# Sliding attention by query blocks of all eight heads, with the values as stationary operand

## The chip, the cores and the metric

The kernel runs on one core of one Trainium2 chip. The metric is the device time of one launch in microseconds. Three runs of the kernel before gave 2348.06 us in the median (2347.34 to 2348.9). A core has TensorE (PE: matmuls and transposes), VectorE (DVE), ScalarE (ACT), GpSimd (POOL) and the DMA queue of SyncE (SP); they work side by side and wait for one another through semaphores. Matmuls read SBUF and write PSUM, of which the kernel uses 8 banks of 128 partitions x 512 fp32.

## The reference

512 tokens of width 1024 go through one block of a first kind and two layers of a second kind. The first block, cut to what the change touches:

```python
qa, ka, va, qb, kb, vb, ga, gb = jnp.split(rmsnorm(x, g) @ w_in, offsets, axis=-1)
oa = dilated_attention(qa, ka, va)              # 12 heads of 64, three dilations
qb = apply_partial_rope(rmsnorm(qb), cos, sin)  # 8 query heads of 64
kb = apply_partial_rope(rmsnorm(kb), cos, sin)  # 2 key heads: four query heads share one
# query block i of 128 sees key blocks i-1 and i, window 128, and a sink logit per head
m = jnp.maximum(jnp.max(s, axis=-1, keepdims=True), sk)
p = jnp.exp(s - m)
denom = jnp.sum(p, axis=-1, keepdims=True) + jnp.exp(sk - m)
o = jnp.einsum('bnjhgqk,bnjkhd->bnjqhgd', p / denom, vb)
mix = sigmoid(ga) * (oa @ w_branch_a) + sigmoid(gb) * (ob @ w_branch_b)
x = x + mix @ w_out                             # then an MLP of width 4096
```

A layer of the second kind is an FFN, a mixer of three branches (stick-breaking attention "sb", a causal softmax attention "mla", a gated linear recurrence "ml") and a second FFN.

## The kernel before

All weight products run with weights and activations split in a high and a low part (three matmuls each, in the format fp32r); attention products and transposes run in fp32. load_w brings weights by SP's DMA (wraw), ScalarE rounds them (whi), VectorE subtracts (wlo).

The order of TensorE is written out by a planner, the class Loom. It carries a model time, now, to which each matmul and transpose adds a fixed price:

```python
self.loom.now += n * 4.17e-4 if rhs.dtype == F32R else 2 * max(0.107, n * 8.34e-4)
```

Attention work is written as jobs that yield either a delay in this model time (T_EXP between scores and transposes, T_PT 1.9 between transposes and value product, T_HEADS 10 and 16 between a projection and the transposes of its heads) or a condition. Between two matmuls of the streamed weight products the planner steps every job that is due. Many conditions ask for room in the slot store H: ND = 18 slots "D" of 4352 bytes a partition, and NB = 5 slots "B" of 2048 bytes, which hold transposed weights (pT in block 1, mpT of mla in block 2) and other small tiles. The order on ScalarE, VectorE, GpSimd and SP is set by the tile scheduler.

Sliding attention is the job swa(tb, kvh): eight units of one query block tb (128 queries) and one key head kvh with its four query heads; the generator attend does most of it. Scores s go to PSUM, VectorE adds the mask and takes the maximum (p), ScalarE forms the exponentials and their sums (den). PE transposes p in pieces of 128x128 (pT), ScalarE and VectorE copy them, and the value product swo has the transposed weights as stationary operand and the values, 64 columns, moving: eight matmuls for two key blocks, four for the first query block. VectorE multiplies the 128x256 result by 1/den, and a second job (o_job) transposes it back (oT), whence ScalarE copies it to ob. Four units wait for kb and qb0, four for kb and qb1. After them come the dilated units (dil_unit), which need the transposed heads q0T and k0T (tile hT) of the projections that run meanwhile.

In block 2 the names are: sbs, the scores of sb; sbl, its triangular sums, with a carry by VectorE between them; sbo, its value product; mls, mlT, mlo: scores, transposes and value product of mla; pf and pt: streamed projections.

Of the kernel before, what the change touches and what calls it, by code (L numbers as in the profile page):

```python
# [9 lines left out]
F32 = mybir.dt.float32  # L10
# [8 lines left out]
D = 1024  # L19
KB = 8  # L20
TB = 4
# [7 lines left out]
def dram(t, off, ap):  # L29
    return bass.AP(tensor=t.tensor, offset=t.offset + off, ap=ap)  # L30
# [96 lines left out]
class Net:  # L127
    def __init__(self, ctx, tc, a):
        self.tc, self.nc, self.a = tc, tc.nc, a
        P = lambda name, bufs, **k: ctx.enter_context(tc.tile_pool(name=name, bufs=bufs, **k))  # L130
        self.const = P("const", 1)
        self.wp = P("wp", 2)
        self.act = P("act", 1)
        self.sc = P("sc", 2)
        self.tiny = P("tiny", 2)
        self.ps = P("ps", 8, space=PSUM)
        ctx.enter_context(tc.manual_schedule(engines={mybir.EngineType.PE}))
        self.loom = Loom()
        self.H = Slots(self.act, [("B", 2048, NB), ("D", 4352, ND)], self.loom.wait)
        self.dr = P("dr", 1, space=bass.MemoryType.DRAM)  # L140
        self.x = self.act.tile([128, KB, S], F32, name="x")
        self.xh = self.act.tile([128, KB, S], F32R, name="xh")
        self.xl = self.act.tile([128, KB, S], F32R, name="xl")
        self.xs = [(self.xh[:, k], self.xl[:, k]) for k in range(KB)]
        self.held = []
        self.normed = False
        self.make_consts()


# [178 lines left out]
            self.hg[n] = t  # L328


    def load_w(self, w, ncol, r0, kb, c0, nc_, c1=None):


        nc = self.nc
        halves = [c0] if c1 is None else [c0, c1]
        w_ = nc_ * len(halves)
        step = max(1, 1024 // w_)
        out = []
        for k0 in range(0, kb, step):
            kn = min(step, kb - k0)  # L340
            raw = self.wp.tile([128, kn * w_], F32, name="wraw", tag="wraw", bufs=WB[0])
            hi = self.wp.tile([128, kn * w_], F32R, name="whi", tag="whi", bufs=WB[1])
            lo = self.wp.tile([128, kn * w_], F32R, name="wlo", tag="wlo", bufs=WB[1])
            rv = raw.rearrange("p (k c) -> p k c", c=w_)
            for i, c in enumerate(halves):
                nc.sync.dma_start(rv[:, :, i * nc_:(i + 1) * nc_],
                                  dram(w, (r0 + k0 * 128) * ncol + c, [[ncol, 128], [128 * ncol, kn], [1, nc_]]))
            nc.scalar.copy(hi, raw)  # L348
            nc.vector.tensor_sub(lo, raw, hi.bitcast(F32))  # L349
            out += [(hi[:, k * w_:(k + 1) * w_], lo[:, k * w_:(k + 1) * w_]) for k in range(kn)]  # L350
        return out
# [279 lines left out]
            nc.scalar.activation(o, ps, AF.Copy, scale=gain)  # L631


    def attend(self, q, k, heads, qs, ks, nb, mask, mcol, dcol, v, ops, sink=None):


        nc = self.nc
        n = nb * 128
        yield lambda: self.H.room(4096)
        p = self.tok("p4")  # L640
        for g in range(2):
            ps = self.bank("s").rearrange("p (h n) -> p h n", n=256)
            for i in range(2):
                h, kv = heads[2 * i + g]
                hs = slice(g * 64, g * 64 + 64)
                self.mm(ps[:, i, 0:n], q[h // 2][hs, qs], k[kv][hs, ks], True, True)
            for i in range(2):
                j = 2 * i + g
                nc.vector.tensor_tensor_reduce(p[:, j, 0:n], ps[:, i, 0:n], mask, scale=0.125, scalar=-3e38,
                                               op0=ALU.add, op1=ALU.max, accum_out=mcol[:, j:j + 1])  # L650
        if sink is not None:
            nc.vector.tensor_max(mcol, mcol, sink)
        nm = self.tiny.tile([128, 4], F32, name="nm", tag="nm", bufs=4)
        nc.vector.tensor_scalar(nm, mcol, -1.0, None, op0=ALU.mult)
        for j in range(4):
            nc.scalar.activation(p[:, j, 0:n], p[:, j, 0:n], AF.Exp, bias=nm[:, j:j + 1], accum_out=dcol[:, j:j + 1])
        if sink is not None:
            e = self.tiny.tile([128, 4], F32, name="es", tag="es", bufs=4)
            nc.vector.tensor_add(e, nm, sink)
            nc.scalar.activation(e, e, AF.Exp)  # L660
            nc.vector.tensor_add(dcol, dcol, e)
        yield T_EXP[nb]
        per = 4 // nb
        yield lambda: self.H.room(2048, 2048)
        pts = []
        for g in range(nb):
            tp = self.bank("pT").rearrange("p (n c) -> p n c", c=128)
            for i in range(4):
                j, b = g * per + i // nb, i % nb
                self.tr(tp[:, i], p[:, j, b * 128:(b + 1) * 128], self.ident)  # L670
            pt = self.blk("pT")
            pts.append(pt)
            if g % 2:
                nc.vector.tensor_copy(pt, tp.rearrange("p n c -> p (n c)"))
            else:
                nc.scalar.copy(pt, tp.rearrange("p n c -> p (n c)"))
        self.H.put(p)
        yield T_PT
        o = ops()
        for g in range(nb):  # L680
            for i in range(4):
                j, b = g * per + i // nb, i % nb
                self.mm(o[:, j], pts[g][:, i * 128:(i + 1) * 128], v(j, b), b == 0, b == nb - 1)
        self.H.put(*pts)

    def o_out(self, o, tb, ys, n):

# [33 lines left out]
    def block1(self):  # L721
        nc, a, T, H, loom = self.nc, self.a, self.tiny, self.H, self.loom
        w = a["w_in"][0]
# [9 lines left out]
        kv = self.tok("kvb")  # L733
# [6 lines left out]
        with self.tc.manual_schedule(engines={mybir.EngineType.DVE, mybir.EngineType.Activation}):  # L740
# [10 lines left out]
            for b in range(TB):  # L751
                ps = self.bank("pt")[:, 0:256]
# [16 lines left out]
        sinks = self.bcast_row(a["sinks"][0], 8, "sinks")  # L769
# [15 lines left out]
        ready = set()  # L785
# [32 lines left out]
        kbT = [kbt[:, 0], kbt[:, 1]]  # L818
        out = {}
# [15 lines left out]
        loom.add(rows_job())  # L835
        two(2304, 2560, 0, ("qb", "qb"), ("qb0", "qb1"))
        ob = [self.duo("ob") for _ in range(2)]
        left = {"swa": 8, "obT": 8, 0: 4, 1: 4, 2: 4}
        units = []

        def swa(tb, kvh):
            nb = 1 if tb == 0 else 2
            ks = slice((tb + 1 - nb) * 128, (tb + 1) * 128)
            m = T.tile([128, 4], F32, name="swm", tag="swm", bufs=4)
            den = T.tile([128, 4], F32, name="swd", tag="swd", bufs=4)
            box = []

            def ops():
                box.append(self.bank("swo").rearrange("p (h d) -> p h d", d=64)[:, 0:4])
                return box[0]  # L850
            qbT = [out[f"qb{i // 2}"][:, i % 2] if i // 2 == kvh else None for i in range(4)]
            yield from self.attend(qbT, kbT, [(h, kvh) for h in range(kvh * 4, kvh * 4 + 4)],
                                   slice(tb * 128, (tb + 1) * 128), ks, nb, self.band[1][:, 256 - nb * 128:256], m, den,
                                   lambda j, b: kv[:, tb + 1 - nb + b, 128 + kvh * 64:192 + kvh * 64], ops,
                                   sinks[:, kvh * 4:kvh * 4 + 4])
            nc.vector.reciprocal(den, den)
            yield lambda: H.room(1024)
            o = H.get("swo", [128, 256])
            nc.vector.tensor_mul(o.rearrange("p (h d) -> p h d", d=64), box[0], den.unsqueeze(2).to_broadcast([128, 4, 64]))

            def done():
                left["obT"] -= 1
            loom.add(self.o_job(o, tb, [ob[kvh]], 2, 2.0, done))
            left["swa"] -= 1
            if left["swa"] == 0:
                H.put(kv, kbt, out.pop("qb0"), out.pop("qb1"))
        for kvh in range(2):
            for tb in range(TB):
                units.append((lambda kvh=kvh: {"kb", f"qb{kvh}"} <= ready, lambda tb=tb, kvh=kvh: swa(tb, kvh)))


        va, og = [], {}
# [99 lines left out]
        wb = a["w_branch_b"][0]  # L972
        for m in range(KB):
            if m % 4 == 0:
                bp = self.load_w(wb, D, 0, 4, m * 128, 512)
            self.after(nc.scalar.activation(mix[m], mix[m], AF.Sigmoid), last)
            pb = self.bank("pbr")
            self.fm(bp, obs, m % 4, pb)
            nc.vector.tensor_mul(mix[m], mix[m], pb)
# [3 lines left out]
        wb = a["w_branch_a"][0]  # L983
        mp = []
        for m in range(KB):
# [3 lines left out]
            if m % 4 == 0:  # L989
                bp = self.load_w(wb, D, 0, 2, m * 128, 512)  # L990
# [618 lines left out]
T_KD, T_HEADS, T_EXP, T_PT = 22.0, (10.0, 16.0), {1: 4.5, 2: 6.5}, 1.9  # L1609
# [30 lines left out]


ND, NB, SCR = 18, 5, 6
WB = (2, 4)
```

## Time and profile before

| | |
|---|---|
| median of three runs | 2348.06 us |
| profiled execution | 2348.01 us |
| its span | 2346.3 us |
| TensorE busy | 2331.9 us, 99% |
| VectorE, ScalarE, GpSimd busy | 1275.5, 905.1, 381.3 us |

The span runs from the first to the last instruction of the profiled execution. Block 1's attention lies in the first 300 us; the mixers of the two layers of block 2 have their attention at about 1000 to 1110 and 1800 to 1910 us. A row of the timeline gives start, duration, engine, line, operation, tile written and tiles read, shapes and the number of merged records. An fp32 matmul or transpose leaves one record or two, by its kind; the x numbers count records.

### The profile page before, as it was taken

To read this page: it belongs to the slowest core of one execution; us is meant where nothing else is said; L and a number is where in the kernel's file an instruction comes from. 1 tells how busy PE (TensorE), PEld (TensorE's weight loads), DVE (VectorE), ACT (ScalarE), POOL (GpSimd) and SP (SyncE) were. 2 spreads that over 40 slices of the span, in tenths; PEclk is the share of its full clock that TensorE was granted. 3 is DMA by queue.
4 is the path that set the end of the run, shared out by engine and by line. 5 is a ranking of instruction groups with operands and counts; after the bars stand their busy time and mean duration, and the time that the engine had idled before them with its cause. 6 is when DMAs were issued, how large, how long until landed. Compare 5 with 4: busy or idle time off the path is not lost.

```text
span 2346.3 us, 28790 instructions
## 1 busy us (share of the span) xinstructions
PE 2331.9 (99%) x11064; PEld 1946.7 (83%) x11064; DVE 1275.5 (54%) x2214; ACT 905.1 (39%) x1510; POOL 381.3 (16%) x385
## 2 busy tenths in 40 slices
PE   8999999999999999999999999999999999999999
PEld 7899888888888888877888888888888778888887
DVE  7744556435355545785554554455458755446552
ACT  6645433222223223676333333223236572333321
POOL 2000014101022112211111321211211110113110
PEclk9999999999999999999999999999999999999999
DMA  4212432333323323322233333333232232323332
GB/s 137 64 55 73 121 96 90 101 97 95 103 86 100 101 92 98 87 65 85 72 90 99 99 95 94 94 95 99 90 101 82 72 86 58 105 81 108 91 102 87
DMA packets 250462, 213.71 MB, mean 91 GB/s; under 512 B 14166, under 2 KB 234068, under 8 KB 250324
## 3 DMA queue, kind: packets, MB, share of 16 engines
q1 hardware_dynamic: 250324, 211.87, 30.4%
q8 instruction: 87, 1.43, 0.2%
q14 instruction: 51, 0.42, 0.1%
HBM read 208.64 MB, written 3.19 MB: 90 GB/s over the span
## 4 chain that ended last, share of the span: by engine, by line
PE 98%; DMA 1%; ACT 0%; DVE 0%; SPq 0%; issue 0%; ACTq 0%
PE pd L175 15%; PE pgate L175 15%; PE pt L175 15%; PE pg L175 10%; PE pa L175 10%; PE pu L175 7%; PE pf L175 6%; PE po L175 5%; PE pbr L175 5%; PE mls L175 1%; PE sbs L175 1%; PE mnum L175 1%; PE sbl L175 1%; PE mss L175 1%; PE mlo L175 1%; PE s L175 1%
## 5 line engine op out<-in xcount | busy, mean ns | idle before, releaser
L349 DVE TENSOR_TENSOR wlo<-wraw,whi 128x1024 fp32r<-128x1024 f32 (+3 forms) x394 | 546.5, 1387 | 415.3 <-ACT whi L348 411.3
L348 ACT CAST whi<-wraw 128x1024 fp32r<-128x1024 f32 (+3 forms) x394 | 404.6, 1028 | 666.7 <-PE pg L175 141.9
L175 PE MATMUL pd<-hidh,whi 128*128 128x512 f32 x520 | 202.3, 389 | 0.0
L175 PE MATMUL pd<-hidl,whi 128*128 128x512 f32 x520 | 202.3, 389 | 0.0
L175 PE MATMUL pd<-hidh,wlo 128*128 128x512 f32 x520 | 202.3, 389 | 0.0
L175 PE MATMUL pgate<-xh,whi 128*128 128x512 f32 x512 | 201.2, 393 | 0.0
L175 PE MATMUL pgate<-xh,wlo 128*128 128x512 f32 x512 | 199.4, 390 | 0.0
L175 PE MATMUL pgate<-xl,whi 128*128 128x512 f32 x512 | 199.3, 389 | 0.0
L175 PE MATMUL pt<-whi,xh 128*128 128x512 f32 (+2 forms) x480 | 182.0, 379 | 0.0
L175 PE MATMUL pt<-whi,xl 128*128 128x512 f32 (+2 forms) x480 | 172.8, 360 | 0.0
L175 PE MATMUL pt<-wlo,xh 128*128 128x512 f32 (+2 forms) x480 | 172.5, 359 | 0.0
L175 PE MATMUL pa<-xl,whi 128*128 128x512 f32 x352 | 137.2, 390 | 0.7 <-DVE xl L438 0.7
L175 PE MATMUL pa<-xh,whi 128*128 128x512 f32 x352 | 137.6, 391 | 0.0
L175 PE MATMUL pg<-xh,whi 128*128 128x512 f32 x352 | 137.4, 390 | 0.0
L175 PE MATMUL pa<-xh,wlo 128*128 128x512 f32 x352 | 137.1, 389 | 0.0
L175 PE MATMUL pg<-xh,wlo 128*128 128x512 f32 x352 | 137.0, 389 | 0.0
L175 PE MATMUL pg<-xl,whi 128*128 128x512 f32 x352 | 137.0, 389 | 0.0
L549 POOL TENSOR_TENSOR t<-t,t 128x512 f32<-128x512 f32 x44 | 56.7, 1290 | 426.5 <-ACT whi L348 303.8
L175 PEld LDWEIGHTS pd<-hidh,wlo 128*128 128x128 f32 x520 | 97.6, 188 | 20.4
L175 PEld LDWEIGHTS pd<-hidl,whi 128*128 128x128 f32 x520 | 97.6, 188 | 20.3
L175 PEld LDWEIGHTS pd<-hidh,whi 128*128 128x128 f32 x520 | 97.6, 188 | 20.1
L175 PEld LDWEIGHTS pgate<-xh,wlo 128*128 128x128 f32 x512 | 96.1, 188 | 20.3
(488 smaller groups left out, 4671.2 us busy)
## 6 DMA issues: line engine op xcount, KB each, us to landing
wraw<-in_w_in_dram SPq DMA_DIRECT2D x116, 512.0 KB, 3.6
wraw<-in_ffn_wi_dram SPq DMA_DIRECT2D x176, 256.0 KB, 3.0
wraw<-in_ffn_wo_dram SPq DMA_DIRECT2D x34, 512.0 KB, 3.5
wraw<-in_w_up_dram SPq DMA_DIRECT2D x32, 512.0 KB, 3.8
wraw<-in_w_out_dram SPq DMA_DIRECT2D x24, 512.0 KB, 3.4
wraw<-in_w_down_dram SPq DMA_DIRECT2D x24, 512.0 KB, 3.9
wraw<-in_w_in_dram SPq DMA_DIRECT2D x32, 256.0 KB, 2.9
wraw<-in_ffn_wo_dram SPq DMA_DIRECT2D x12, 384.0 KB, 3.1
```

The lines of the kernel that those rows point to most:

```text
L175: self.nc.tensor.matmul(out, lhsT, rhs, start=start, stop=stop)
L348: nc.scalar.copy(hi, raw)
L349: nc.vector.tensor_sub(lo, raw, hi.bitcast(F32))
L549: nc.gpsimd.tensor_mul(t2, t2, t1)
```

## The change

Sliding attention becomes four units, one for each query block, with all eight heads (the new method weigh does scores and exponentials, turned the transposes and their copy, which goes to ScalarE and VectorE in turn). VectorE multiplies the weights p by 1/den before they are transposed. The value product takes the values (128x64) as stationary operand and the transposed weights, 512 columns of four heads, as the moving one; key head 0 writes partitions 0 to 63 and key head 1 partitions 64 to 127 of one bank, in turn. The result stands transposed, so the transposes oT and their job are gone and ScalarE copies it to ob. Since ob now has its rows in another order, load_w brings the rows of w_branch_b in two halves of 64 partitions (eight DMAs of half the size for four). A unit waits for kb, qb0 and qb1. NB goes from 5 to 9, for the whole program.

```diff
+            if part:
+                for i in range(2):
+                    nc.sync.dma_start(rv[i * 64:i * 64 + 64],
+                                      dram(w, (r0 + i * part + k0 * 64) * ncol + c0, [[ncol, 64], [64 * ncol, kn], [1, nc_]]))
+                halves = []
...
+    def turned(self, p, jb):
+
+        nc = self.nc
+        tp = self.bank("pT").rearrange("p (n c) -> p n c", c=128)
+        for i, (j, b) in enumerate(jb):
+            self.tr(tp[:, i], p[:, j, b * 128:(b + 1) * 128], self.ident)
+        pt = self.blk("pT")
+        self.odd = not self.odd
+        (nc.scalar.copy if self.odd else nc.vector.tensor_copy)(pt, tp.rearrange("p n c -> p (n c)"))
+        return pt
...
-        def swa(tb, kvh):
+        def swa(tb):
...
-            nc.vector.reciprocal(den, den)
-            yield lambda: H.room(1024)
-            o = H.get("swo", [128, 256])
-            nc.vector.tensor_mul(o.rearrange("p (h d) -> p h d", d=64), box[0], den.unsqueeze(2).to_broadcast([128, 4, 64]))
-
-            def done():
-                left["obT"] -= 1
-            loom.add(self.o_job(o, tb, [ob[kvh]], 2, 2.0, done))
+            for kvh in range(2):
+                yield lambda: H.room(4096)
+                m = T.tile([128, 4], F32, name="swm", tag="swm", bufs=4)
+                den = T.tile([128, 4], F32, name="swd", tag="swd", bufs=4)
+                q = [out[f"qb{kvh}"][:, i % 2] for i in range(4)]
+                p = self.weigh(q, kbT, [(h, kvh) for h in range(kvh * 4, kvh * 4 + 4)], ts, ks, nb,
+                               self.band[1][:, 256 - nb * 128:256], m, den, sinks[:, kvh * 4:kvh * 4 + 4])
+                nc.vector.reciprocal(den, den)
+                pv = p[:, :, 0:nb * 128]
+                nc.vector.tensor_mul(pv, pv, den.unsqueeze(2).to_broadcast([128, 4, nb * 128]))
+                ps.append(p)
+                yield 1.0
+            yield T_EXP[nb] + 1.0
+            yield lambda: H.room(*[2048] * (2 * nb))
+            pts = [[self.turned(p, [(j, b) for j in range(4)]) for b in range(nb)] for p in ps]
+            H.put(*ps)
+            yield T_PT
+            o = self.bank("swo")
+            for b in range(nb):
+                for kvh in range(2):
+                    c = 128 + kvh * 64
+                    self.mm(o[kvh * 64:kvh * 64 + 64], kv[:, tb + 1 - nb + b, c:c + 64], pts[kvh][b], b == 0, b == nb - 1)
+            H.put(*sum(pts, []))
+            for i in range(2):
+                nc.scalar.copy(ob[i][:, :, ts], o[:, i * 256:i * 256 + 256].rearrange("p (n c) -> p n c", c=128))
...
-            units.append((lambda kvh=kvh: {"kb", f"qb{kvh}"} <= ready, lambda tb=tb, kvh=kvh: swa(tb, kvh)))
+            units.append((lambda: {"kb", "qb0", "qb1"} <= ready, lambda tb=tb: swa(tb)))
...
-                bp = self.load_w(wb, D, 0, 4, m * 128, 512)
+                bp = self.load_w(wb, D, 0, 4, m * 128, 512, part=256)
...
-ND, NB, SCR = 18, 5, 6
+ND, NB, SCR = 18, 9, 6
```

The order on TensorE moves at two kinds of places. The first is in block 1, where the heads of the first dilation, q0 and k0 (tile qk), are transposed into hT. Before, at the end of the sliding units of the second key head:

```order
L175 MATMUL pt<-whi,xl 128x256
L182 MATMUL pT<-ident,p_1166 128x128 x4
L175 MATMUL swo<-kvb,pT 128x64 x8
L175 MATMUL s<-kbT,qb1T 128x256 x4
L175 MATMUL swo<-kvb,pT 128x64 x4
L175 MATMUL s<-kbT,qb1T 128x256 x4
L182 MATMUL hT<-ident,qk 128x128 x16
```

Five of the eight units' value products have been done by then. Now, with only the first of four units done (swo x2 is its value product, the x4 that of the second):

```order
L176 MATMUL swo<-pT,kvb 64x512 x2
L176 MATMUL s<-kbT,qb0T 128x256 x4
L183 MATMUL pT<-ident,p_918 128x128 x8
L183 MATMUL pT<-ident,p_978 128x128 x8
L176 MATMUL s<-kbT,qb1T 128x256 x4
L183 MATMUL hT<-ident,qk 128x128 x8
L176 MATMUL swo<-pT,kvb 64x512 x4
L176 MATMUL s<-kbT,qb0T 128x256 x4
L183 MATMUL hT<-ident,qk 128x128 x8
```

The transposes of q0 moved ahead of the second unit's value product, and no streamed matmul stands among these rows.

The second place is in the mixers of block 2, the same in both layers: the last query block of mla (its scores mls, transposes mlT, value products mlo) beside the second head pair of sb. Before, on TensorE:

```order
L175 MATMUL mlo<-mv,mpT 128x64 x4
L175 MATMUL mls<-mhT 128x512
L175 MATMUL mlo<-mv,mpT 128x64 x3
L175 MATMUL pt<-whi,xh 128x512
L175 MATMUL pt<-wlo,xh 128x512
L175 MATMUL pt<-whi,xl 128x512
...
L182 MATMUL mlT<-ident,mp 128x128 x4
```

Behind the dots three more streamed matmuls stand, and from there on the transposes, value products and sums come singly, each with six or more streamed matmuls (pt) between. Now, from the last scores of sb's second head pair to the last value product of mla:

```order
L176 MATMUL sbs<-sbq,sbk 128x512
L183 MATMUL mlT<-ident,mp 128x128 x12
L176 MATMUL pf<-xh,whi 128x512
...
L176 MATMUL mlo<-mv,mpT 128x64 x4
L176 MATMUL mls<-mhT 128x512
L176 MATMUL mlo<-mv,mpT 128x64 x8
L183 MATMUL oT<-ident,mo 128x128 x2
L183 MATMUL mlT<-ident,mp 128x128 x4
L176 MATMUL sbl<-sbp,trigt 128x128
L176 MATMUL sbl<-sbp_8593,trigt 128x256
L176 MATMUL mlo<-mv,mpT 128x64 x4
```

Behind the dots stand eleven more matmuls of pf; three heads are transposed at once, and the value products, scores and sums behind pf follow one another with no streamed matmul between.

## Rows read from the trace of the kernel before

**Rows 1.** The page: the span, busy time by engine, the chain's shares by engine.
```profile
span 2346.3 us, 28790 instructions
...
PE 2331.9 (99%) x11064; PEld 1946.7 (83%) x11064; DVE 1275.5 (54%) x2214; ACT 905.1 (39%) x1510; POOL 381.3 (16%) x385
...
PE 98%; DMA 1%; ACT 0%; DVE 0%; SPq 0%; issue 0%; ACTq 0%
```

**Rows 2.** All that TensorE waited for: total us, times, longest us.
```profile
PE colT L182 <- DMA rows<-in_ln_g_dram: 4.7, 1, 4.7
PE xtp L182 <- DMA xin<-in_x_dram: 4.0, 1, 4.0
PE pa L175 <- DVE xl L438: 0.7, 1, 0.7
PE po L175 <- DVE mxl L527: 0.6, 1, 0.6
PE pT L182 <- ACT q0T L631: 0.2, 1, 0.2
```

**Rows 3.** Timeline of TensorE (start us, duration us), block 1's sliding attention.
```profile
80.58 1.89 PE L175 MATMUL swo<-kvb,pT 128*128 128x64 f32 x16
82.40 1.14 PE L175 MATMUL s<-kbT,qb0T 64*128 64x256 f32 x8
...
101.09 1.97 PE L182 MATMUL hT<-ident,qk 128*128 128x128 f32 x16
```

**Rows 4.** Timeline of TensorE, the stick-breaking value product of layer 1.
```profile
1033.48 0.39 PE L175 MATMUL pf<-xh,wlo 128*128 128x512 f32 x1
1033.80 2.37 PE L175 MATMUL sbo<-sbz,sbv 128*64 128x512 f32 x16
1036.10 2.42 PE L175 MATMUL sbs<-sbq,sbk 64*128 64x384 f32 x8
```

**Rows 5.** Timeline of TensorE, one fp32 score matmul of 512 columns (mls).
```profile
1058.29 1.08 PE L175 MATMUL mls<-mhT 96*128 96x512 f32 x2
1059.21 0.78 PE L175 MATMUL mlo<-mv,mpT 128*128 128x64 f32 x6
```

**Rows 6.** Timeline of TensorE, a pair of transposes back among streamed matmuls.
```profile
92.57 0.38 PE L182 MATMUL oT<-ident,swo 128*128 128x128 f32 x2
92.70 0.36 PE L175 MATMUL pt<-whi,xh 128*128 128x256 f32 x1
92.91 0.28 PE L175 MATMUL pt<-wlo,xh 128*128 128x256 f32 x1
```

**Rows 7.** Timeline of VectorE, q0's normalising product and its last rotary step.
```profile
91.95 1.22 DVE L791 TENSOR_TENSOR qk<-qk,rh16y 128x1024 f32<-128x1024 f32 x1
...
94.14 0.42 DVE L622 TENSOR_TENSOR qk<-ru,rv 128x256 f32<-128x256 f32 x1
```

**Rows 8.** Timeline of ScalarE, layer 1: an sb exponential; the score copies' start; mla's exponential.
```profile
1031.87 1.05 ACT L1411 ACTIVATE sbz<-sbz 128x1024 f32<-128x1024 f32 x1
...
1037.33 0.60 ACT L1380 ACTIVATE sbz<-sbs 128x512 f32<-128x512 f32 x1 [0.50 <-PE sbs L175]
...
1042.29 0.54 ACT L1319 ACTIVATE mp<-mp,mnm 128x256 f32<-128x256 f32 x1
```

**Rows 9.** Timelines of TensorE and VectorE: a triangular sum and its carry.
```profile
1026.13 0.81 PE L175 MATMUL sbl<-sbp,trigt 128*128 128x384 f32 x2
...
1027.24 0.54 DVE L1405 TENSOR_TENSOR sbp<-sbl,sbt 1x384 f32<-1x384 f32 x1
```

**Rows 10.** Timeline of TensorE after the wait that ends at 10.88 us.
```profile
14.35 0.41 PE L175 MATMUL pt<-whi,xl 128*128 128x256 f32 x1
14.56 0.41 PE L175 MATMUL pt<-whi,xh 128*128 128x256 f32 x1
...
15.15 0.28 PE L175 MATMUL pt<-whi,xh 128*128 128x256 f32 x1
15.26 0.28 PE L175 MATMUL pt<-wlo,xh 128*128 128x256 f32 x1
```

More of the change, by code (lines that the diff above doesn't have):

```diff
@@ L146, in __init__ @@
         self.normed = False
+        self.odd = False
         self.make_consts()
@@ L328, in rope2, with load_w @@
             self.hg[n] = t
-    def load_w(self, w, ncol, r0, kb, c0, nc_, c1=None):
+    def load_w(self, w, ncol, r0, kb, c0, nc_, c1=None, part=None):
         nc = self.nc
@@ L631, in heads_T, with weigh @@
             nc.scalar.activation(o, ps, AF.Copy, scale=gain)
-    def attend(self, q, k, heads, qs, ks, nb, mask, mcol, dcol, v, ops, sink=None):
+    def weigh(self, q, k, heads, qs, ks, nb, mask, mcol, dcol, sink=None):
         nc = self.nc
         n = nb * 128
-        yield lambda: self.H.room(4096)
         p = self.tok("p4")
@@ L661, in attend @@
             nc.vector.tensor_add(dcol, dcol, e)
+        return p
+    def turned(self, p, jb):
[7 more added lines that the diff above has]
+        return pt
+    def attend(self, q, k, heads, qs, ks, nb, mask, mcol, dcol, v, ops):
+        H = self.H
+        yield lambda: H.room(4096)
+        p = self.weigh(q, k, heads, qs, ks, nb, mask, mcol, dcol)
         yield T_EXP[nb]
         per = 4 // nb
[L664 to L677, printed above, removed]
+        yield lambda: H.room(2048, 2048)
+        self.odd = False
+        pts = [self.turned(p, [(g * per + i // nb, i % nb) for i in range(4)]) for g in range(nb)]
+        H.put(p)
         yield T_PT
@@ L683, in attend @@
                 self.mm(o[:, j], pts[g][:, i * 128:(i + 1) * 128], v(j, b), b == 0, b == nb - 1)
-        self.H.put(*pts)
+        H.put(*pts)
     def o_out(self, o, tb, ys, n):
@@ L837, in block1 @@
         ob = [self.duo("ob") for _ in range(2)]
-        left = {"swa": 8, "obT": 8, 0: 4, 1: 4, 2: 4}
+        left = {"swa": 4, 0: 4, 1: 4, 2: 4}
         units = []
-        def swa(tb, kvh):
+        def swa(tb):
             nb = 1 if tb == 0 else 2
             ks = slice((tb + 1 - nb) * 128, (tb + 1) * 128)
[L844 to L855, printed above, removed]
-            nc.vector.reciprocal(den, den)
-            yield lambda: H.room(1024)
-            o = H.get("swo", [128, 256])
-            nc.vector.tensor_mul(o.rearrange("p (h d) -> p h d", d=64), box[0], den.unsqueeze(2).to_broadcast([128, 4, 64]))
-            def done():
-                left["obT"] -= 1
-            loom.add(self.o_job(o, tb, [ob[kvh]], 2, 2.0, done))
@@ new lines, in swa @@
+            ts = slice(tb * 128, (tb + 1) * 128)
+            ps = []
+            for kvh in range(2):
+                yield lambda: H.room(4096)
+                m = T.tile([128, 4], F32, name="swm", tag="swm", bufs=4)
[8 more added lines that the diff above has]
+                yield 1.0
@@ L866, in swa @@
                 H.put(kv, kbt, out.pop("qb0"), out.pop("qb1"))
-        for kvh in range(2):
-            for tb in range(TB):
-                units.append((lambda kvh=kvh: {"kb", f"qb{kvh}"} <= ready, lambda tb=tb, kvh=kvh: swa(tb, kvh)))
+        for tb in range(TB):
+            units.append((lambda: {"kb", "qb0", "qb1"} <= ready, lambda tb=tb: swa(tb)))
         va, og = [], {}
```

## The prediction

> **What bounds the kernel now.** I read the page's busy times and chain first [rows 1]: TensorE is busy 99% of the span and makes up 98% of the chain that ended last; VectorE is busy 54%. Then the list of what TensorE waited for [rows 2]: five entries, 10.2 us together, 8.7 of them the first loads of the program; in the mixers of block 2 there is none. So the time is the sum of TensorE's work, and the change can help only by taking work from it and can hurt only by making it wait. The profiled execution took 2348.01 us, 1.71 us more than its span, and the median of the three runs is 2348.06; I add to 2348.0.
>
> **Work that goes.** The value product before is 56 matmuls of 64 columns, two records each. Sixteen records take 1.82 us [rows 3], so the 112 cost 112/16 x 1.82 = 12.7 us. After, it is 14 matmuls of 512 columns, in 7 pairs: the key heads write the two halves of a bank's partitions. The program of before has the same form once per layer and pair of heads, the stick-breaking value product: 8 matmuls with stationary values of 128x64, alternating between the halves, 2560 columns in all, take 2.30 us from start to start of the next group [rows 4]. That is 1280 pair columns at 1.80 ns. A single stream of 512 fp32 columns takes 0.92 us, also 1.80 ns a column [rows 5], so the two of a pair ran side by side. Seven pairs of 512 columns then cost 3584 x 1.80 ns = 6.4 us, and with 0.09 us at each of four entries (1033.80 against the usual 0.23 us behind 1033.48, [rows 4]) 6.7 us. That is **-6.0 us**; the bounds are -6.3 (no entries) and 0 (no overlap, below).
>
> The same rows bear on a rule against the change: entry and exit of this form showed about 0.1 us. The Trainium skill, "TensorEngine Tiling (Array Packing)", Key Properties, says that a change of tiling mode drains the TensorE. By that rule the four units pay at both ends, for which the page has no price; by the row it is the 0.1 us above.
>
> The transposes back go: eight pairs. A pair puts the third matmul behind it 0.34 us after its own start, where one streamed matmul of 256 columns alone would have taken 0.12 [rows 6]: 0.22 us a pair, **-1.75 us**. The copies to ob stay eight in number, now without the transposes ahead of them.
>
> **VectorE.** Eight products of 128x256 become two of 128x512 and six of 128x1024; one of 128x1024 takes 1.22 us [rows 7]. VectorE gets some 5 us more of work within 40 us and has room for it, so this costs only where TensorE stands behind it. It now lies between the exponentials and the transposes. For the first unit the transposes of the second key head wait about 0.4 us for it, and its value product about 0.3 us for ScalarE's copy, which stands behind exponentials: +0.7 us (0 to 1.5). The alternation of copies between ScalarE and VectorE shifts one copy.
>
> **The first dilated heads.** The order charges a model time for each matmul: 0.214 us for one of 64 columns and 0.854 for one of 512, so 12.0 us for either form, though the new one takes half. What is timed by this clock therefore comes too early. The transposes of q0 (hT) stand at 101.09 before [rows 3]; in the new order less work is ahead of them: 32 narrow value matmuls at 0.228, less the one 0.9 us pair of the first unit, 6.4 us; 12 streamed matmuls of 256 columns at 0.12, 1.4; eight transposes, 0.9; four score matmuls, 1.1; six transposes back, 0.7. That is 10.4 to 10.5 us, so they are due at 90.7. But q0 is finished on VectorE by the row at 94.14 [rows 7], at about 94.5; its norms start from projections that stand where they stood, and its chain now shares VectorE with the normalising products, so I take 95.0. With the 0.7 of above TensorE arrives at 91.4 and waits 3.6 us (2 to 4.5: the lower end if the scheduler serves q0 first, the upper if a product of 1.22 is ahead of it). Behind it stands the second unit's value product, whose last weights VectorE copies only after k0's product (1.22) and its own wait: about +0.95 us (0 to 1.5). Afterwards 24 and more streamed matmuls stand between steps, and I find no wait. **+5.3 us** in all. Block 1 then comes out at -6.0 - 1.75 + 5.3 = -2.5 us (-6 to 0). The loads of w_branch_b, 8 halves for 4, are followed by matmuls that cover them, and SP has nothing urgent behind them: 0.
>
> **Block 2, by the small slots.** NB = 9 belongs to the whole program. In both layers jobs that waited for a B slot (the transposed weights of mla) now run at once, and the order becomes denser: groups of fp32 work stand next to one another instead of between streamed matmuls. The work is the same; what changes is how long each producer has. I followed the new order with the durations of before. The clearest place is the second stick-breaking head. Its score matmuls take 2.4 us [rows 4], twelve transposes 1.2 and twelve streamed matmuls 2.75, so mlo is due 6.3 us after the scores start. ScalarE begins copying the scores 1.23 us after they start and is occupied for 4.96 us (1037.33 to 1042.29, [rows 8]); in the new order two exponentials, one the 1.05 us one of [rows 8], end only at about 1.8 us, and the copy of the transposed weights (0.6, as the copies there) stands behind all this: ready at 7.4, a wait of **1.1 us** (0 to 1.5). The next exponential of mla stands behind it too, with only mlo and one transpose pair ahead of its own transposes: 1.2 (0.5 to 1.6). The two carry matmuls of 128 and 256 columns stand back to back, though the second needs a sum of the first's result; by the 384-column one before [rows 9] that sum ends 1.65 us after its matmul began, 0.8 of it the matmul itself: 0.95 (0.6 to 1.5). The first stick-breaking value product comes before its exponential (behind a cast and a subtraction) and the mask on GpSimd: 0.75 (0 to 1.2). The first dense transposes and mlo behind the first head's ScalarE block: 0.65 and 0.5 (0 to 1 each). Together 5.15, call it **+5 us a layer** (2 to 7), **+10 us** for the two. The fewer changes between streamed and fp32 matmuls I count at nothing: before, a visit costs hardly more than its work [rows 6].
>
> **Sum.** 2348.0 - 6.0 - 1.75 + 5.3 + 10 = 2355.5; I say **2355 us**, with 2351 to 2359 for this case itself.
>
> **Rivals.** (1) Block 2 covers itself: the producers are early, as in all of before, where no such wait shows [rows 2]. Against it speaks that the order of before has streamed matmuls between just these steps. Time: 2348.0 - 2.5, 2345.5, within 0.2%; with half the waits 2350. (2) Block 1's waits don't come either, q0 being ready when asked: 2348.0 - 7.75, 2340. That needs q0 4 us earlier than before, for which I see no reason. (3) The pairs don't overlap: 14 x 0.92 = 12.9 us for the value product, nothing gained there, 2361. For it speaks only that the new kernel streams 512 columns of transposed weights at once; against it [rows 4]. (4) The clock: after the 4.0 us wait at the start, matmuls of 256 columns ran 0.21 us apart until 15.0 and 0.11 to 0.12 afterwards [rows 10]; half the pitch is the lower of the levels 1.2 and 2.4 GHz, though the page grants 1.00 there on average. If the 3.6 us at q0 did the same, four us at half speed cost 2 us more: 2357. (5) VectorE meets the normalising products first and q0 comes later still: decided where two of them stand ahead of q0's product, 2 x 1.22, so +2.4: 2358.
>
> **How the numbers follow.** Waits in block 2 and block 1 (with 4 and 5, which lie in its range) 0.54; block 2 covered or half covered 0.28; all covered, or block 1's waits and block 2's both under half, 0.13; pairs not overlapping 0.05. A measurement of this kernel can tell about 0.2%, 4.7 us, from no change: faster is under 2343.3, slower over 2352.7. Faster takes the 0.13 and a little of the second case, 0.15. Slower takes the pairs' 0.05 and all but 0.07 of the forecast's 0.54 (its lower bounds), 0.52; the rest, 0.33, is within. The range reaches from 2342, which leaves out most of the all-covered case, to 2361, the case without overlap.
>
> **What the profile will show.** Value matmuls of 64x512 in four groups of 1.0, 1.9, 1.9 and 1.9 us, a half of it each if I am right on the pairs; a wait of hT for VectorE's qk of 2 to 4.5 us near 91 us; the rows from the dilated attention on some 2.5 us earlier than before; in the list of waits mlo, mlT, sbl and sbo against ScalarE, VectorE and GpSimd, 2 to 7 us a layer. Wrong is the forecast if that list has under 2 us a layer in block 2; then the sum is 2348 less block 1's gain. It is also wrong if block 1 ends later than before.

## The result, and the profile after

The changed kernel took **2368.19 us** (median of four runs, 2366.75 to 2369.68) against 2348.07 us for the kernel before on the same chip: a ratio of 1.0086 [1.007, 1.0102], 20.1 us more. The forecast was 2355, at most 2361. The direction was right and the size was not, and the time lies outside the range. The profiled execution took 2369.54 us, 21.5 more than that of before.

The page of the changed kernel (span; busy time, share and instructions by engine; the chain's shares by engine), which answers to [rows 1]:

```profile
span 2367.8 us, 28577 instructions
...
PE 2341.1 (99%) x10964; PEld 1942.5 (82%) x10964; DVE 1282.5 (54%) x2215; ACT 905.9 (38%) x1509; POOL 378.2 (16%) x385
...
PE 96%; DVE 1%; ACT 1%; DMA 1%; issue 0%; SPq 0%; ACTq 0%; DVEq 0%
```

TensorE has 100 matmul records fewer and is yet busy 9.2 us longer; its idle time (span less busy) grew by 12.3. So besides the waits, matmuls that were not changed must take longer. TensorE's waits (total us, times, longest), without the first loads' two, which answer to [rows 2]:

```profile
PE mlo L176 <- ACT mpT L1351: 3.6, 4, 1.3
...
PE mlT L183 <- ACT mp L1340: 3.1, 4, 1.2
PE sbl L176 <- DVE sbp L1426: 2.6, 2, 1.3
PE hT L183 <- DVE qk L629: 2.4, 1, 2.4
...
PE pT L183 <- DVE swm L654: 0.9, 1, 0.9
PE hT L183 <- ACT q0T L638: 0.8, 1, 0.8
PE pT L183 <- DVE p L870: 0.7, 1, 0.7
```

Those in mlo, mlT and sbl are block 2's, in two layers alike: 9.3 us; hT and pT are block 1's, 4.7. All were in the forecast, about as large.

Where the stages begin divides the loss. The tile rows give count, durations, and first and last start (us). Before:

```profile
L175 PE MATMUL pu<-xh,whi x256: 388/389/486, 386.9 to 681.4; 128*128 128x512 f32 x128
L175 PE MATMUL po<-msh,whi x128: 389/389/389, 1313.5 to 2157.0; 128*128 128x512 f32 x128
```

After:

```profile
L176 PE MATMUL pu<-xh,whi x256: 389/389/486, 385.3 to 679.9; 128*128 128x512 f32 x128
L176 PE MATMUL po<-msh,whi x128: 389/389/389, 1323.5 to 2178.7; 128*128 128x512 f32 x128
```

The first pu stands behind block 1: 386.9 to 385.3, 1.6 us earlier (0.7 of that is shorter waits for the first loads). The first po stands behind layer 1's mixers and the last behind layer 2's: +11.6 and +11.7 us. **The changed attention gains a little; the two mixers, which the diff does not touch except through the slot count, lose 11.7 us each**, where the forecast had 5.

Why more than their waits is in TensorE's timeline in layer 1 (start, duration, then idle before and releaser):

```profile
1032.11 3.33 PE L176 MATMUL sbo<-sbz,sbv 128*64 128x512 f32 x16
1035.36 2.42 PE L176 MATMUL sbs<-sbq,sbk 64*128 64x384 f32 x8
...
1068.10 1.10 PE L176 MATMUL mlo<-mv,mpT 128*128 128x64 f32 x8 [1.30 <-ACT mpT L1351]
1069.04 1.47 PE L176 MATMUL mls<-mhT 96*128 96x512 f32 x2
1070.31 3.52 PE L176 MATMUL mlo<-mv,mpT 128*128 128x64 f32 x16
...
1075.42 1.11 PE L183 MATMUL mlT<-ident,mp 128*128 128x128 f32 x4 [1.17 <-ACT mp L1340]
...
1078.26 1.19 PE L176 MATMUL sbl<-sbp,trigt 128*128 128x256 f32 x2 [1.29 <-DVE sbp L1426]
```

The mls matmul of 512 columns that took 0.92 us to the next start [rows 5] takes 1.27 here. The granted clock of this stretch and of the fp32 work ahead of it (window; us, busy; clock; DMA share; GB/s):

```profile
1055.00:1060.00 5.00, 5.00 (x22) 1.00 0.50 157
...
1068.10:1069.10 1.00, 1.00 (x9) 1.00 0.00 0
1069.10:1072.00 2.90, 2.90 (x12) 0.59 0.00 0
...
1079.00:1083.00 4.00, 4.00 (x15) 0.50 0.26 66
1083.00:1086.00 3.00, 3.00 (x13) 0.96 0.00 0
```

From about 1.5 us after the first of the three waits until 1083.2, 13.6 us in all, TensorE ran at the lower of its two levels (0.50: 1.2 instead of 2.4 GHz); two more waits fell into that time.

### The profile page after: what moved, and what is told of

Its sections match the earlier page's. It is cut to its first block, busy times and chain, and to the rows that moved or that the text cites. A ratio compares the mean times of both kernels' runs of the same rounds, so it can differ in the third digit from the quotient of the medians.

```text
span 2367.8 us, 28577 instructions
## 1 busy us (share of the span) xinstructions
PE 2341.1 (99%) x10964; PEld 1942.5 (82%) x10964; DVE 1282.5 (54%) x2215; ACT 905.9 (38%) x1509; POOL 378.2 (16%) x385
## 4 chain that ended last, share of the span: by engine, by line
PE 96%; DVE 1%; ACT 1%; DMA 1%; issue 0%; SPq 0%; ACTq 0%; DVEq 0%
PE pgate L176 15%; PE pd L176 15%; PE pt L176 14%; PE pg L176 10%; PE pa L176 10%; PE pu L176 7%; PE po L176 6%; PE pf L176 5%; PE pbr L176 5%; PE mlo L176 1%; PE mls L176 1%; PE mnum L176 1%; PE mss L176 1%; PE sbl L176 1%; PE dio L176 1%; PE s L176 1%
## 5 line engine op out<-in xcount | busy, mean ns | idle before, releaser
L176 PEld LDWEIGHTS pd<-hidh,wlo 128*128 128x128 f32 x520 | 97.6, 188 | 20.1
```

Source lines behind the costliest of these rows:

```text
L176: self.nc.tensor.matmul(out, lhsT, rhs, start=start, stop=stop)
```

## The experiments

**The slot count alone, both ways.** NB is the one number that the attention and the mixers share. Taken back in the kernel after (e1), and set in the kernel before (e2):

```diff
-ND, NB, SCR = 18, 9, 6
+ND, NB, SCR = 18, 5, 6
```

```diff
-ND, NB, SCR = 18, 5, 6
+ND, NB, SCR = 18, 9, 6
```

> The changed kernel with the small slots back at 5, nothing else. Its order on TensorE differs from that of before in block 1 alone and from that of after in block 2 alone. Theory (block 2 lost 11.7 us a layer, by waits and by the clock behind them, and the slots alone made its order; block 1 gained 1.7 us): 2346.4 us, no waits of mlo, mlT or sbl, clock 1.00 in both mixers. Rival (the new form of block 1 loads the chip so that the clock falls later, or the swap costs elsewhere): still over 2360 us, with a clock under 1.00 after 1000 us.

> The kernel of before with 9 small slots, nothing else: block 1 by the old units, block 2 in the dense order of after. Theory: 2348.1 + 2 x 11.7 = 2371.5 us, with the same waits (mlo 1.3, mlT 1.2, sbl 1.3 us a layer) and a clock of 0.94 from 1000 to 1110 us. Rival (the dense order is harmless without the new form of block 1): 2348 us.

Measured: e1 2347.2 us, ratio 0.9998 [0.9989, 1.0007]; e2 2368.76, 1.0091 [1.0077, 1.0105]. The new attention with the old slot count is no slower than before; the old attention with the new count carries the whole loss. TensorE's waits in e2, without any change to the attention, are nearly those of after. Behind them stands the clock of layer 1's mixers in e2:

```profile
PE mlo L175 <- ACT mpT L1330: 3.6, 4, 1.3
PE mlT L182 <- ACT mp L1319: 3.5, 4, 1.6
PE sbl L175 <- DVE sbp L1405: 2.8, 2, 1.5
...
1000.00:1110.00 110.00, 104.61 (x506) 0.97 0.22 65
```

So +21 us belong to NB in block 2, and the attention itself is worth -0.6 us in block 1, which the interval does not tell from nothing. The expected clock of 0.94 came in e2's layer 2 alone; in layer 1 it is 0.97, the lower level lasting half as long. By the starts of pu and po that layer lost 9.7 us, where after, with much the same waits, lost 11.6.

**Waits or clock: matmuls that fill the three waits.** In the kernel after, matmuls without use, into banks that the next step overwrites, keep TensorE at work where it would wait (e3). One of the three places was met by both pairs of heads, though only the second waits there, so e3 does 6 matmuls a layer too many; in e5 its condition is (kb, hf, pr) == (2, 1, 1). The three places stand ahead of mlT's transposes, mlo and sbl, in this order of the diff.

```diff
+    def fill(self, out, n):
+        for _ in range(n):
+            self.nc.tensor.matmul(out, self.onesr, self.xh[:, 0], start=True, stop=True)
+            if (tb, h) == (3, 3):
+                self.fill(tp, 5)
+            if (tb, h) == (3, 0):
+                self.fill(opb, 6)
+            if (kb, hf) == (2, 1):
+                self.fill(pl[2], 6)
```

> The changed kernel, order unchanged, with 5 or 6 streamed matmuls of 512 columns (1.1 to 1.4 us), whose result is overwritten, in front of the three longest waits of each layer of block 2 (mlo of the last query block, mlT behind it, the second carry sum): the data come as late as before, but TensorE works meanwhile. Theory (the clock falls because TensorE stands idle for 3.8 of 12 us): the waits shrink to 0.3 us or less, no stretch at half pitch follows, 2368.2 - 2 x 6.7 = 2354.8 us (2353 to 2358 with some filler to spare). Rival (the dense fp32 work itself, not the idle time, lowers the clock): the half pitch stays from 1068 to 1083 us and the time is 2367 to 2371 us.

> As e3_fill_block2, without the six filling matmuls that stood there by oversight also in front of the first head pair's carry sum (no wait there, 1.4 us a layer for nothing). What e3 told: the clock stays at 1.00, but TensorE then comes sooner to each late operand, so the three places cost 1.5, 1.8 and 1.8 us instead of 1.3, 1.2 and 1.3. Theory (the clock's net price is some 3.7 us a layer, the waits at full clock some 6.9): 2363.6 - 2.8 = 2360.8 us. Rival (the clock's price is the 5.6 us a layer by which the slow rows are longer): 2357 us.

Measured: e3 2363.63, ratio 1.0068 [1.0054, 1.0081]; e5 2360.77, 1.0057 [1.0044, 1.007]. The two differ by 2.9 us, 0.24 for each of the 12 matmuls too many. The clock stays whole in both layers. The window of layer 1's mixers in e5, and then in the kernel after:

```profile
1000.00:1110.00 110.00, 108.55 (x536) 1.00 0.23 70
```

```profile
1000.00:1110.00 110.00, 105.28 (x498) 0.94 0.21 61
```

In e5 streamed fillers stand between the fp32 groups too, so e5 alone would not tell idle time from dense fp32 work. The kernel after does: from 1053.6 to 1063.8 us its fp32 groups follow one another with no streamed matmul and no wait between, and the clock there is 1.00 (from 1055 to 1060 above). So dense fp32 work by itself did not lower the clock; it fell where idle time came in among such work. And the price divides: 2368.2 - 2360.8 = 7.4, **3.7 us a layer for the clock**; 2360.8 - 2347.2 (e1) = 13.6, **6.8 a layer for the waits** themselves. (Each run taken against the kernel before in its own comparison, which moved by up to 0.6 us, the two are 3.4 and 7.0.) Most of the latter is in e5's timeline:

```profile
1067.27 1.56 PE L184 MATMUL mlo<-xh,onesr 128*128 128x512 f32 x6
1068.73 1.10 PE L176 MATMUL mlo<-mv,mpT 128*128 128x64 f32 x8
...
1072.46 1.40 PE L184 MATMUL mlT<-xh,onesr 128*128 128x512 f32 x5
1074.28 0.66 PE L187 MATMUL mlT<-ident,mp 128*128 128x128 f32 x4 [0.42 <-ACT mp L1345]
1074.92 1.64 PE L184 MATMUL sbl<-xh,onesr 128*128 128x512 f32 x6
1076.71 0.67 PE L176 MATMUL sbl<-sbp,trigt 128*128 128x256 f32 x2 [0.15 <-DVE sbp L1437]
```

From start to start with the rest of the wait the three places cost 1.46, 1.82 and 1.79 us, where after shows 1.30, 1.17 and 1.29: a TensorE at full speed arrives sooner and waits longer for the same producers. That is why the slow stretch costs less than its rows say. From 1068.10 to 1083.40 the kernel after takes 15.30 us, 12.84 without its two waits; e5 does the same work in 7.2 (from 1068.73 to 1079.5, less fillers and waits). So 5.7 us more at the lower clock, of which some two hide producers' time.

**Can delays make nine slots good?** The order's delays could be set to the denser order: the transposes of mla's weights, its value products and the sb carry due later (e9; T_EXP + 5.0 concerns block 1, below).

```diff
-T_MLA, T_MP, T_MPT = {"q": 12.0, "k": 5.0}, 3.0, 2.4
-T_SB, T_SBR, T_SBW = 9.0, 1.5, 2.0
+T_MLA, T_MP, T_MPT = {"q": 12.0, "k": 5.0}, 5.0, 5.0
+T_SB, T_SBR, T_SBW = 9.0, 3.0, 2.0
-            yield T_EXP[nb] + 1.0
+            yield T_EXP[nb] + 5.0
```

> The changed kernel with 9 small slots kept, but longer delays in the order's model time: 5.0 instead of 3.0 and 2.4 us between the steps of mla, 3.0 instead of 1.5 between the carry sums, and the 4 us of e6 in block 1. In block 2 streamed matmuls stand again between the steps of the last query blocks, though not between all. Theory (the 5 slots only held the steps apart; the delays were too short for the producers): 2340.8 us as e6 plus what dense places are left, 2341 to 2345, clock 1.00, waits under 2 us a layer. Rival (more slots in flight crowd ScalarE and VectorE whatever the delays): over 2350 us.

Measured: 2363.07, ratio 1.0061 [1.0049, 1.0073]. The theory fell. e6, below, has the same block 1 with five slots and took 2340.84: against it e9 loses 22.2 us, 11 a layer, about as much as after, so what e9 gains on after is block 1's. The three waits left the list, and another step took their place. The longest entry of block 2 in e9's list of waits:

```profile
PE sbl L176 <- POOL sbp L1416: 6.4, 4, 2.8
```

A triangular sum now comes before GpSimd's step on sbp, and the clock is 0.95 in both layers. Whether some other set of delays suits nine slots stays open.

**Block 1: q0 asked for later, and its waits filled.** With five slots, only block 1 differs from before. TensorE's rows there in the kernel after:

```profile
94.97 0.66 PE L183 MATMUL hT<-ident,qk 128*128 128x128 f32 x4 [2.35 <-DVE qk L629]
96.40 0.78 PE L183 MATMUL hT<-ident,qk 128*128 128x128 f32 x4 [0.78 <-ACT q0T L638]
97.11 3.46 PE L176 MATMUL swo<-pT,kvb 128*64 128x512 f32 x8
100.50 1.95 PE L176 MATMUL s<-kbT,qb0T 64*128 64x256 f32 x8
...
113.67 1.94 PE L176 MATMUL swo<-pT,kvb 128*64 128x512 f32 x8
115.54 0.72 PE L176 MATMUL s<-k0T,q0T 64*128 64x128 f32 x8
```

The value product of a unit takes 1.87 us to the next start at 113.67 and 3.39 at 97.11, behind the waits for q0. e4 asks for q0 and k0 4 us later; e8 puts filling matmuls ahead of q0's transposes, 10 for the first bank and 3 for the second. Both have NB = 5; e4's edit, then e8's:

```diff
-                yield delay
+                yield delay + (4.0 if key in ("q0", "k0") else 0.0)
```

```diff
+            self.fill(ps, fill[p])
...
-                self.heads_T(t, [o[:, 0], o[:, 1]], self.hg[tab])
+                self.heads_T(t, [o[:, 0], o[:, 1]], self.hg[tab], (10, 3) if key == "q0" else (0, 0))
```

> The changed kernel with 5 small slots, and q0's and k0's transposes asked for 4 us of model time later: they move behind 12 streamed matmuls and the second unit's value product. Theory (in block 1 the waits of hT, 2.35 and 0.78 us, and the half pitch behind them, 2.4 us, take back most of the gain): 2346.4 - 5.5 = 2341 us, hT waits under 0.3 us, swo of the second unit 1.9 us instead of 3.5. Rival (the work that replaces the wait only moves it to the next step, k0 or the scores of the dilated heads): 2344 to 2346 us, with a wait of that length there.

> The changed kernel with 5 small slots and 10 and 3 streamed matmuls of 512 columns, whose result is overwritten, in front of q0's two groups of transposes (2.3 and 0.7 us, about the waits of 2.4 and 0.8 there). Theory (the idle time there brings the half pitch of 97 to 100.5 us): full pitch, swo of the second unit 1.9 us and not 3.5, 2347.2 - 2.3 = 2344.9 us. Rival (the fp32 work with columns in pairs does): the half pitch stays, 2347 us.

Measured: e4 2346.44, ratio 0.9995 [0.9986, 1.0004]; e8 2345.75, 0.9992 [0.9983, 1.0]. In e4 hT waits only 0.2 us, but TensorE reaches the next unit's transposes sooner and waits there. The longest entry of its waits in block 1, and the window of block 1's attention:

```profile
PE pT L183 <- DVE p L870: 2.6, 2, 1.9
...
60.00:135.00 75.00, 70.69 (x433) 1.00 0.18 56
```

With 0.9 at another pT and 0.7 at swo they are 4.4 us instead of 4.7: the wait was moved, not removed, and the expected 2341 missed. The clock stayed 1.00 for all that: waits of this length are not always followed by the lower level. In e8 the same value product, behind filled waits, runs at full pitch again, though the fillers themselves wait 1.1 us:

```profile
94.85 2.60 PE L184 MATMUL hT<-xh,onesr 128*128 128x512 f32 x10 [1.12 <-DVE pT L682]
...
99.20 1.94 PE L176 MATMUL swo<-pT,kvb 128*64 128x512 f32 x8
101.07 1.14 PE L176 MATMUL s<-kbT,qb0T 64*128 64x256 f32 x8
```

1.87 us to the next start for 3.39, at a clock that in after was

```profile
97.10:100.50 3.40, 3.40 (x10) 0.54 0.00 0
100.50:102.40 1.90, 1.90 (x11) 1.00 0.00 0
```

The scores at 100.50 in after, 1.88 us for the 1.07 of the same group in e8, are not the clock's: it is back at 1.00, and the group's eight records stand one after another there, two at a time in e8. e8 gains 1.4 us against e1, whose interval (0.9989 to 1.0007) is wider than that: the timeline shows the clock's part in block 1, the times alone would not.

**The normalising product left out, and asked for later.** e7 takes VectorE's products away to see whether they hold up block 1. e6 keeps them and makes the transposes of the normalised weights due 4 us later. Both have NB = 5; e7's edit, then e6's:

```diff
-                pv = p[:, :, 0:nb * 128]
-                nc.vector.tensor_mul(pv, pv, den.unsqueeze(2).to_broadcast([128, 4, nb * 128]))
```

```diff
-            yield T_EXP[nb] + 1.0
+            yield T_EXP[nb] + 5.0
```

> The changed kernel with 5 small slots, the product of the weights with 1/den left out (the result is then not normalised); the order on TensorE is the same. Theory (the normalising product stands on the path of the transposes and delays q0 on VectorE): the waits of pT, 0.7 and 0.9 us, shrink to under 0.3 each, that of hT from 2.4 to about 1.5, 2347.2 - 2.5 = 2344.7 us. Rival (VectorE has room, the waits come from the exponentials and from q0's own chain): the waits stay, 2346.5 to 2347 us.

> The changed kernel with 5 small slots and 4 us more of model time between a sliding unit's scores and its transposes; nothing else. 48 streamed matmuls of 256 columns move ahead of the first unit's transposes, so these, q0's and k0's come some 5.7 us later. Theory (block 1's waits come from delays that leave out VectorE's normalising product and q0's chain): no wait over 0.5 us in block 1, no half pitch, 2347.2 - 4.7 - 2.3 = 2340 us. Rival (as in e4, each wait only moves on to the next late operand): 2344 to 2347 us.

Measured: e7 2347.59, ratio 0.9999 [0.9991, 1.0008]; e6 **2340.84, 0.9971 [0.996, 0.9982]**. Without the products TensorE's waits in block 1 are hardly fewer (4.1 us for 4.7), and the time is that of e1. e7 waits 2.1 and 0.8 us at hT, 0.9 at swo and 0.3 at pT. The window of its attention in block 1:

```profile
60.00:135.00 75.00, 70.91 (x429) 0.95 0.19 57
```

The clock is 0.95 here and 0.98 in e1: the lower level lasted about 7 us instead of some 3. So the two times differ in more than the products, and e7 does not settle what these cost.

With later transposes other work stands ahead of every one of the late steps. All that TensorE waits for in e6's attention:

```profile
PE swo L176 <- DVE pT L677: 0.3, 1, 0.3
```

The waits of block 1 are gone but for 0.3 us, and the granted clock between 60 and 135 us is 1.00 (after: 0.98). e6 is faster than both kernels: 6.6 us under before.

**Two halves in turn, or one after the other.** The forecast priced the value product by supposing that two matmuls into opposite halves of a bank run side by side. e10 is e6 with the loops exchanged, so that matmuls into the same half follow one another.

```diff
-            for b in range(nb):
-                for kvh in range(2):
+            for kvh in range(2):
+                for b in range(nb):
```

> The kernel of e6 with the value matmuls of a unit in another order: both key blocks of key head 0, then both of key head 1, so that only the middle two of four stand next to one of the other half of the partitions. Theory (two neighbours that write different halves run side by side, each at 0.92 us for 512 columns): three of four steps show, 2.8 us a unit instead of 1.9, three units, 2340.8 + 2.7 = 2343.5 us. Rival (matmuls of 64 stationary columns take half the time whatever stands beside them): 2340.8 us, 1.9 us a unit. Second rival (only the strict alternation pairs): 3.7 us a unit, 2346.3 us.

Measured: 2339.96, ratio 0.9966 [0.9954, 0.9978], as e6. The theory missed, and by the time alone the first rival would have it. TensorE's records say otherwise. A matmul of this kind leaves two records; in e10's unit of four matmuls the first two pairs of records (windows 116.90:117.10 and 117.40:117.60), then what follows the unit, are:

```profile
116.72 0.66 PE L176 MATMUL swo<-pT,kvb 128*64 128x512 f32 x2
117.19 0.60 PE L176 MATMUL swo<-pT,kvb 128*64 128x512 f32 x2
...
118.59 0.72 PE L176 MATMUL s<-k0T,q0T 64*128 64x128 f32 x8
```

The records run two at a time, 1.87 us for the four matmuls, as with the halves in turn (113.67, above). Both weight loads of the first pair wait for ScalarE and both of the third for VectorE; ScalarE copied the transposed weights of the first key block and VectorE those of the second, for either key head. So a pair is one matmul of each half, although the program issues both of the first half ahead of both of the second. What a half does alone is seen in the kernel after, in block 2's sbo at 1032.11, the same form (windows 1032.20:1032.40 and 1032.75:1033.00, then the weight loads, PEld):

```profile
1032.11 0.64 PE L176 MATMUL sbo<-sbz,sbv 128*64 128x512 f32 x1
1032.59 0.59 PE L176 MATMUL sbo<-sbz,sbv 128*64 128x512 f32 x1
...
1033.06 0.20 PEld L176 LDWEIGHTS sbo<-sbz,sbv 128*64 128x64 f32 x4 [0.77 <-POOL sbz L1435]
```

Until GpSimd's mask for the other half came, at 1033.06, one record ran at a time: 0.95 us for a matmul of 512 columns with 64 stationary ones, no less than one with 128 takes (0.92, [rows 5]). So the first rival falls, and the forecast's premise stands: two matmuls into opposite halves run side by side. What fell is that they must be issued in turn. The Trainium skill, "TensorEngine Tiling (Array Packing)", Key Properties, says that different tiles can run matmuls in parallel; the trace agrees (x2 above).

## Why the prediction was wrong

- **What bounds the kernel:** right. TensorE makes up 96% of the chain after, and every microsecond is its work, its waits or its clock.
- **Work that goes, -6.0 and -1.75:** right in size. The four units took 1.0 us (86.11 to 87.11, the one of two matmuls) and three times 1.87 at full clock, 6.6 in all for the 6.7 of the forecast. The reason given, two matmuls of a pair side by side, holds (e10), so rival 3 did not come; that the halves need the alternation is not borne out. The transposes back were not measured apart; e6, without waits, has 6.6 us of the 7.75.
- **VectorE and q0, +5.3:** near. The waits came to 4.7 us (0.7 and 0.9 at pT, 2.35 and 0.8 at hT), and q0's transposes began at 94.97, forecast 95.0. What the normalising products delay stays open: without them 0.6 us of waits goes, and the time, at a clock lower for longer, is the same (e7). What holds TensorE is that these steps are asked for when less work stands ahead of them; due later, they wait for nothing (e6). That the order's charge of 12.0 us for the product makes q0 early was not run.
- **Block 1's clock (rival 4):** it came, near the size given there. The value product behind q0 took 3.39 for 1.87, 1.5 us more; it was set at 2 and kept out of the likeliest sum. The scores behind it took 0.8 more at full clock, their records one after another, which the forecast did not have. Block 1 is then -6.1 - 1.75 + 4.7 + 1.5 + 0.8, about -0.9; e1 says -0.6, the forecast said -2.5.
- **Block 2, +5 a layer:** the places were right, and the sizes as the profile shows them: mlo 0.48 and 1.30 (0.5 and 1.1), mlT 0.38 and 1.17 (0.65 and 1.2), sbl 1.29 (0.95, where its own 1.65 less 0.8 is 0.85); sbo is no entry in the list, but took 3.25 us to the next start for 2.30 [rows 4], about 1.0 (0.75), since one half of it came late from GpSimd (1033.06, above). That is 5.6 for 5.15.
- **The step that failed** is the price of block 2, +5 us a layer, which stopped at the sum of these waits and put the clock at nothing there. Rival 4 knew from [rows 10] that a wait can halve the clock and allowed for it at q0 alone. In block 2 the stretch of 13.6 us at the lower clock adds 5.7 us a layer to the rows, 11.3 with the waits, of the 11.7 that the stages lost. The runs divide it otherwise: 6.8 for the waits at full clock and 3.7 net for the lower one. With 3.7 a layer and rival 4's two microseconds the forecast's sum would have been 2365, and with the waits at 6.8 a layer too, 2368.5.
- **Chances:** "slower" had 0.52. The range ended at 2361, the case without overlap, because no case had block 2 above 7 us a layer. Rival 1 (block 2 covers itself) fell with e2; rivals 2 and 5 did not come, though e6 shows rival 2's 2340 is to be had when the steps are asked for later.

## What to carry to other kernels

A slot count that a whole program shares paces stages that the change never names: set it alone in the old kernel first, and look where the order moves. When work between hand-ordered steps goes, later due times give its gain back (6.6 us here), provided that the step behind is looked at too: asked for later, one step's wait passed to its neighbour. And price a wait on a busy TensorE with the clock that it may cost, at every place where such waits come and not only at the longest.

## What was not expected of the hardware

- **A wait of 1.30 us was followed by 13.6 us at half clock** (1069.6 to 1083.2, granted 0.50), with two more waits of 1.17 and 1.29 inside; at q0, 2.35 and 0.78 us of waiting were followed by about 3.4 us. With the waits filled by useless matmuls the granted clock stayed 1.00 there (e5, e8). It also stayed 1.00 in e4's block 1, with 4.4 us of waits, the longest 1.9: what decides it, these runs do not tell.
- **The lower clock costs less than it shows:** 5.7 us a layer by the rows, 3.7 by the times, since part of it is time in which producers catch up.
- **Two fp32 matmuls into opposite halves of a bank ran side by side though the program issued both of one half first** (e10: four of 512 columns in 1.87 us, two records at a time). With one half late, a matmul of the other ran alone and took 0.95 us (sbo at 1032.11), a wait that stands in no list of TensorE's waits.
